# Down-projection products in another order, a buffer of its own for a weight sum, eight raw weight buffers, and gate/up low parts on VectorE instead of by DMA

## The chip, the cores and the metric

The kernel runs on one core of a Trainium2 chip. The metric is the device time of one execution in microseconds, taken as the median of several runs. The engines are TensorE (PE in the profile, its weight loads PEld), VectorE (DVE), ScalarE (ACT), GpSimd (POOL) and SyncE (SP); each runs its own instructions strictly in the order in which they stand in the program.

## The reference

The model is a trunk of two layers over 512 tokens of width 1024. A layer is a half-weighted SwiGLU block (FFN), a token-mixing block, and another FFN. Only the FFN is touched by the change:

```
def swiglu(x, w_gate_up, w_down):
    g, u = jnp.split(x @ w_gate_up, 2, axis=-1)
    return (jax.nn.silu(g) * u) @ w_down

x = x + 0.5 * swiglu(rms_norm(x, ffn1_norm[l]), ...)     # 1024 -> 2 x 2816 -> 1024
x = x + token_mixing(rms_norm(x, mix_norm[l]), ...)
x = x + 0.5 * swiglu(rms_norm(x, ffn2_norm[l]), ...)
```

The work is done to float32 accuracy: a product of two float32 matrices is made of three matmuls in a reduced format, high part by high part, high by low, and low by high.

## The kernel before

**Who orders the instructions.** A scheduler in Python runs when the kernel is built. Every piece of work is a task that yields instructions with a priority and a guessed cost and waits for events; the scheduler simulates the engines and writes each engine's instructions in the order of its simulation. On the chip that order is fixed; semaphores are put in from the tiles that instructions read and write.

**Weights.** `Stream` brings all weights of the FFNs and of the mix stage as units of 128x1024. SyncE loads a unit into one of RAWB raw buffers (`wraw`), and it is cut into a high part `whi` and a low part `wlo`, for which there are CUTB = 3 pairs of buffers. A pair comes free when TensorE has done the product that uses it, a raw buffer when the unit has been cut. For a gate/up or mix unit ScalarE writes the negative of the raw weights, rounded to the reduced format, into `wlo` (L357) and the high part into `whi` (L358), and GpSimd issues a DMA that adds the raw weights to `wlo` (L359). For a unit of the down-projection ScalarE makes the high part (L363) and VectorE subtracts it from the raw weights (L364).

**An FFN.** The 22 chunks of 128 hidden columns are done in three blocks of 8, 8 and 6 (`BLOCKS`). For a chunk, gate and up are 8 x 3 matmuls of 128x512 each into a bank psa (L502 to L504). After a block its part of the down-projection follows: two quads, q0 and q1, each for four of the eight output tiles of x. A quad is a two-by-two block product by the Strassen-Winograd scheme: seven products p0 to p6 instead of eight, each of one weight unit (weights or sums of weights) with one *form* of the hidden pairs. A pair is two chunks; the forms of a pair (`Pair.make`) are cut into high and low parts in the order 0, then 3 and 4, 5 and 6, and last 2 and 1. A product takes, for each of the 4 (in the third block 3) pairs, 6 matmuls of 128x256 (L693, L695, L696). The products accumulate in three banks: z in pst, y in pso, x in pss. Since the sums of the scheme nest, z is used by four products one after the other and is read after each.

**The weight sums.** `sums` and `third` make the combinations of the four weight quarters: a GpSimd DMA adds one quarter to another in a raw buffer (L302, L319), VectorE adds two buffers (L306, L311).

**Reading the accumulators** (`evac` in `down`). ScalarE copies the accumulators of the first three products (L761, L767, L771) and so lets the next product use the bank; VectorE adds the copies to x (L756). The last four are added from PSUM directly (L756 too). After the last block each finished x tile starts the next norm: high part by ScalarE (L555), low part by VectorE (L556), square by ScalarE, sum of squares on GpSimd (L572).

Of the kernel before, what the change touches and what calls it, by code (L numbers as in the profile page):

```python
# [12 lines left out]
F32 = mybir.dt.float32  # L13
# [7 lines left out]
P = 128  # L21
S = 512
# [16 lines left out]
           gc=9288)  # L39
RAWB, CUTB = 6, 3  # L40
NSLOT = 58
# [18 lines left out]
NHU = PLAN.count("s")  # L60
QUADS = [e for e in PLAN if e != "s"]

# [34 lines left out]
class Event:  # L97
    def __init__(self):
        self.done = False
        self.waiting = []  # L100
# [127 lines left out]
class Unit:  # L228


    def __init__(self, w=1024, plain=None):
        self.w, self.plain = w, plain
        self.src, self.ev = Event(), Event()
        self.raw = self.hi = self.lo = None


class Stream:
# [5 lines left out]
    def __init__(self, nc, sch, pool, wall, wq):  # L243
        self.nc, self.s, self.pool, self.wall, self.wq = nc, sch, pool, wall, wq
        self.order, self.avail = [], 0
        self.raw, self.cut = Res(RAWB), Res(CUTB)
        self.units, self.plain, self.quads = [], [], {}
        for e in PLAN:
            if e == "s":
                u = Unit(plain=len(self.plain))  # L250
                self.plain.append(u)
                self.units.append(u)
            else:
                self.quads[e] = [Unit(quad_width(e)) for _ in range(7)]
                self.units += self.quads[e]

    def task(self, gate):
        self.s.spawn(self._cutter(), -1e6)
        n = 0
        for e in PLAN:  # L260
            if e == "s":
# [32 lines left out]
    def _quad(self, e):  # L294
        i, w = QUADS.index(e), quad_width(e)
        u11, us1, us2, u12, us3, us4, u22 = self.quads[e]
        w11, w12, w21, w22 = (self.wq[i, k][:, :w] for k in range(4))
        V, O, s, prio = self.nc.vector, self.nc.gpsimd, self.s, -1e6 + 10 * i

        def sums(t11, t22, t12):  # L300
            yield 1.0
            yield "pool", 0.9, lambda: O.dma_start(t22, w21, accum_op=ALU.add), {}  # L302
            yield 5.0
            s.set(us1.src)
            yield us1.ev
# [3 lines left out]
            yield us2.ev  # L309
            yield u12.ev  # L310
            yield DVE(w, lambda: V.tensor_add(t22, t22, t12), ap=1)  # L311
            s.release(self.raw)
            s.set(us4.src)
            yield us4.ev
            s.release(self.raw)

        def third(t11):
# [3 lines left out]
            s.set(us3.src)  # L321
            yield us3.ev
            s.release(self.raw)

        def last():
            yield u22.ev
# [7 lines left out]
        s.spawn(sums(u11.raw, us1.raw, u12.raw), prio)  # L334
        u22.raw = yield from self._load(w22)
        self._later(u22.src, 2.0)
        s.spawn(last(), prio)

# [8 lines left out]
    def _cut(self, k, u):  # L347
        A, V, O = self.nc.scalar, self.nc.vector, self.nc.gpsimd
        if u.plain == 0:
            for i in range(4):  # L350
# [4 lines left out]
                yield 0.6  # L355
        elif u.plain is not None:
            yield ACT(u.w, lambda: A.mul(u.lo, u.raw, -1.0))  # L357
# [4 lines left out]
        else:  # L362
            yield ACT(u.w, lambda: A.copy(u.hi, u.raw))  # L363
            yield DVE(u.w, lambda: V.tensor_sub(u.lo, u.raw, u.hi.bitcast(F32)), ap=1)  # L364
        if u.plain is not None:
            self.s.release(self.raw)
# [26 lines left out]
def trunk_kernel(ctx: ExitStack, tc: tile.TileContext, wall, wq, x_in, pos_in, cols_in, out):  # L393
# [235 lines left out]
    class Pair:  # L629
# [8 lines left out]
        def make(self, a, b):  # L638
# [14 lines left out]
            for src, i, j in ((t, 3, 4), (u, 5, 6), (b, 2, 1)):  # L653
# [7 lines left out]

    STEPS = ((0, 0, "z", True), (1, 3, "y", True), (2, 5, "z", False), (3, 1, "x", True), (4, 4, "z", False),
             (5, 2, "y", False), (6, 6, "z", False))

    def quad(e, pairs, evac, prio):
# [7 lines left out]
        def product(i):  # L673
            iu, form, z, begin = STEPS[i]
            u, H = units[iu], S // 2
            before = [j for j in range(i) if STEPS[j][2] == z]
            yield u.ev
# [31 lines left out]
    def ffn(name, l, u, xs, nxt):  # L709
# [38 lines left out]
        def down(b, q, was, prio):  # L748
# [9 lines left out]
            def evac(acc, done, seen):  # L758
                q1, q5, uu = G(), G(), G()
                yield done[0]  # L760
                yield ACT(S, lambda: A.copy(q1, acc["z"]))  # L761
                sch.set(seen[0])
                for ev in was:
                    yield ev
                yield add(x11, q1, 0.5)
                yield done[1]
                yield ACT(S, lambda: A.copy(q5, acc["y"]))  # L767
                sch.set(seen[1])
                yield add(x22, q5, -0.5)
                yield done[2]  # L770
                yield ACT(S, lambda: A.copy(uu, acc["z"]))  # L771
                sch.set(seen[2])
                yield add(x12, uu, 0.5)
                yield done[3]
                yield add(x11, acc["x"], 0.5, bump=EVAC)
                sch.release(banks[QBANK["x"]])
                yield done[4]
                yield add(x22, acc["z"], -0.5, bump=EVAC)
                sch.set(seen[4])
                yield done[5]  # L780
                yield add(x12, acc["y"], 0.5, bump=EVAC)
                sch.release(banks[QBANK["y"]])
                last = b == len(BLOCKS) - 1
                for r in range(2):
                    m = 4 * q + r
                    if last:
                        sch.set(new[m][1])
                        nxt.add(m, new[m][0], prio + r)
                yield done[6]
                yield add(x21, acc["z"], -0.5, bump=EVAC)  # L790
                sch.release(banks[QBANK["z"]])
                for r in range(2, 4):
                    m = 4 * q + r
                    if last:
                        sch.set(new[m][1])
                        nxt.add(m, new[m][0], prio + r)

# [44 lines left out]
    def mix(l, u, xs, nxt):  # L842
# [11 lines left out]
        def v_task():  # L854
            kinds = ["a", "a", "t", "o"]
            for k in range(KT - 1):
                yield u.u[k].ev
# [28 lines left out]
            for t in range(NB):  # L886
                p = vp[t]
                p.h = gp.tile([P, 256], F32R, name="vh", tag="vh", bufs=NB)
                p.lo = gp.tile([P, 256], F32R, name="vl", tag="vl", bufs=NB)
                rt = u.tok[:, t:t + 1]  # L890
# [512 lines left out]
```

## Time and the profile before

| | before |
|---|---|
| median of 3 runs | 2984.92 us (2982.92 to 2985.18) |
| profiled execution | 2984.55 us, span 2982.8 us |
| TensorE busy | 2874.0 us, 96% |
| ScalarE busy | 1541.4 us, 52% |
| VectorE busy | 1430.8 us, 48% |
| GpSimd busy | 791.6 us, 27% |
| mean granted TensorE clock | 0.984 of full speed |

The profiled execution is one of many and lies within the spread of the runs. Busy times are sums over the span. A matmul counts as busy until its modelled end, which overlaps the start of the next. The clock is a share of 2.4 GHz; the granted levels are 1.2 and 2.4 GHz.

### The profile page before, as it was taken

The page shows a single profiled execution, that of the slowest core. Times are in us where ns is not written, and L with a number is a line of the kernel's source. Part 1 is how long each engine was busy: PE and PEld are TensorE (multiplying, and loading weights), DVE is VectorE, ACT ScalarE, POOL GpSimd, SP SyncE. Part 2 cuts the span into 40 slices and gives each one's busy share as a digit, 9 for nine tenths or more (in the row PEclk, how much of TensorE's full clock was granted, in tenths as well). Part 3 has the DMA queues.
Part 4 walks back from the last instruction along what each step waited for, and adds up shares of the span by engine and source line. Part 5 has one row for each costly group of instructions (what it writes and reads, how often), then busy time and mean ns, then how long its engine had stood idle before and what let it go on. Part 6 is the DMA issues. An engine that isn't in the chain of part 4 may idle for free.

```text
span 2982.8 us, 36980 instructions
## 1 busy us (share of the span) xinstructions
PE 2874.0 (96%) x14304; PEld 2407.7 (81%) x14304; DVE 1430.8 (48%) x2371; ACT 1541.4 (52%) x2076; POOL 791.6 (27%) x795
## 2 busy tenths in 40 slices
PE   8999989899999999999999999999999999999997
PEld 6888878678888888888878888877788888888886
DVE  5835568954313223535635356599352221235545
ACT  5544457666534455444454444566665334544444
POOL 2111155633222231111220111646242222311111
PEclk9999999899999999999999999998999999999998
DMA  8686677576688888687686865866757888877773
GB/s 218 161 195 167 150 186 162 131 158 155 141 189 189 187 191 186 162 180 171 145 186 167 186 170 136 205 139 141 162 135 163 186 193 184 190 179 171 172 182 84
DMA packets 141233, 503.51 MB, mean 169 GB/s; under 512 B 15681, under 2 KB 16321, under 8 KB 141057
## 3 DMA queue, kind: packets, MB, share of 16 engines
q0 software_dynamic: 65600, 236.75, 43.9%
q1 hardware_dynamic: 74736, 263.23, 28.1%
q8 instruction: 113, 1.85, 0.3%
q10 hardware_dynamic: 720, 1.17, 0.1%
q14 instruction: 64, 0.52, 0.1%
HBM read 285.60 MB, written 2.10 MB: 96 GB/s over the span
## 4 chain that ended last, share of the span: by engine, by line
PE 78%; DVE 11%; issue 6%; DMA 3%; POOL 1%; ACT 1%; SPq 0%; DVEq 0%; POOLq 0%; ACTq 0%
PE psa L504 23%; PE psa L502 22%; PE psa L503 22%; DMA wlo<-wraw 3%; DVE g L949 2%; DVE m L948 2%; PE pst L693 1%; PE pst L696 1%; PE pst L695 1%; DVE g L1034 1%; DVE g L974 1%; DVE wlo L364 1%; DVE g L1014 1%; PE pso L696 1%; DVE wraw L306 1%
## 5 line engine op out<-in xcount | busy, mean ns | idle before, releaser
L502 PE MATMUL psa<-g,whi 128*128 128x512 f32 x3216 | 1283.4, 399 | 37.9 <-DVE xr L969 15.5
L504 PE MATMUL psa<-g,wlo 128*128 128x512 f32 x3216 | 1280.6, 398 | 20.2 <-DMA wlo<-wraw 20.2
L503 PE MATMUL psa<-g,whi 128*128 128x512 f32 x3216 | 1278.7, 398 | 0.3 <-DVE g L556 0.3
L357 ACT ACTIVATE wlo<-wraw 128x1024 fp32r<-128x1024 f32 x407 | 431.4, 1060 | 911.4 <-PE psa L504 860.7
L502 PEld LDWEIGHTS psa<-g,whi 128*128 128x128 f32 x3216 | 611.0, 190 | 185.7 <-DVE xr L969 9.2
L504 PEld LDWEIGHTS psa<-g,wlo 128*128 128x128 f32 x3216 | 610.6, 190 | 171.3 <-DMA wlo<-wraw 26.4
L503 PEld LDWEIGHTS psa<-g,whi 128*128 128x128 f32 x3216 | 610.7, 190 | 140.9 <-DVE g L556 1.3
L359 POOL DMA_DIRECT2D wlo<-wraw x407 | 353.6, 869 | 1319.6 <-ACT wlo L357 1207.7
L358 ACT CAST whi<-wraw 128x1024 fp32r<-128x1024 f32 x407 | 420.8, 1034 | 0.0
L363 ACT CAST whi<-wraw 128x1024 fp32r<-128x1024 f32 (+1 forms) x168 | 159.8, 977 | 228.4 <-PE psa L503 97.1
L693 PE MATMUL pst<-g,whi 128*128 128x256 f32 x704 | 203.7, 289 | 18.9 <-ACT g L761 17.1
L696 PE MATMUL pst<-g,wlo 128*128 128x256 f32 x704 | 200.7, 285 | 5.7 <-DVE wlo L364 5.7
L695 PE MATMUL pst<-g,whi 128*128 128x256 f32 x704 | 200.9, 285 | 0.0
L364 DVE TENSOR_TENSOR wlo<-wraw,whi 128x1024 fp32r<-128x1024 f32 (+1 forms) x168 | 186.1, 1133 | 29.0 <-ACT whi L363 28.9
L733 DVE TENSOR_TENSOR g<-psa,g 128x512 f32<-128x512 f32 x88 | 60.8, 691 | 252.7 <-PE psa L504 252.5
L724 DVE TENSOR_TENSOR g<-psa,g 128x512 f32<-128x512 f32 x88 | 60.8, 691 | 235.7 <-PE psa L504 235.6
L693 PEld LDWEIGHTS pst<-g,whi 128*128 128x128 f32 x704 | 134.9, 192 | 25.0 <-ACT g L761 20.2
L696 PEld LDWEIGHTS pst<-g,wlo 128*128 128x128 f32 x704 | 135.0, 192 | 6.5 <-DVE wlo L364 6.5
L695 PEld LDWEIGHTS pst<-g,whi 128*128 128x128 f32 x704 | 135.2, 192 | 0.6
L656 DVE TENSOR_TENSOR g<-g 128x512 fp32r<-128x512 f32 x132 | 90.8, 688 | 47.5 <-ACT g L655 47.5
L319 POOL DMA_DIRECT2D wraw<-in_wq_dram x24 | 20.8, 867 | 345.0 <-DVE wraw L306 192.2
L696 PE MATMUL pso<-g,wlo 128*128 128x256 f32 x352 | 100.1, 284 | 5.9 <-DVE wlo L364 5.9
(222 smaller groups left out, 3258.8 us busy)
## 6 DMA issues: line engine op xcount, KB each, us to landing
wraw<-in_w_dram SPq DMA_DIRECT2D x407, 512.0 KB, 4.5
wlo<-wraw POOLq DMA_DIRECT2D x407, 512.0 KB, 5.9
wraw<-in_wq_dram SPq DMA_DIRECT2D x64, 512.0 KB, 4.6
wraw<-in_wq_dram POOLq DMA_DIRECT2D x32, 512.0 KB, 7.0
wraw<-in_wq_dram SPq DMA_DIRECT2D x32, 384.0 KB, 3.5
wraw<-in_wq_dram POOLq DMA_DIRECT2D x16, 384.0 KB, 5.7
x<-in_x_dram SPq DMA_DIRECT2D x8, 256.0 KB, 4.7
out_dram<-g ACTq DMA_DIRECT2D x4, 256.0 KB, 2.9
```

Of the source, the lines that this page charges most:

```text
L357: yield ACT(u.w, lambda: A.mul(u.lo, u.raw, -1.0))
L358: yield ACT(u.w, lambda: A.copy(u.hi, u.raw))
L359: yield "pool", 0.9, lambda: O.dma_start(u.lo, u.raw, accum_op=ALU.add), {}
L363: yield ACT(u.w, lambda: A.copy(u.hi, u.raw))
L364: yield DVE(u.w, lambda: V.tensor_sub(u.lo, u.raw, u.hi.bitcast(F32)), ap=1)
L502: T.matmul(ps, wh, xh, start=first, stop=False)
L503: T.matmul(ps, wh, xl, start=False, stop=False)
L504: T.matmul(ps, wl, xh, start=False, stop=last)
L656: yield DVE(S, lambda: V.tensor_sub(lo, src, h.bitcast(F32)))
L693: T.matmul(o, u.hi[:, c], xh, start=begin and k == 0 and m == 0, stop=False, skip_group_check=True)
L695: T.matmul(o, u.hi[:, c], xl, start=False, stop=False, skip_group_check=True)
L696: T.matmul(o, u.lo[:, c], xh, start=False, stop=k == n - 1 and m == 1, skip_group_check=True)
```

## The change

There are four parts. The raw buffers become eight. Plan letters tell mix units ("m", cut as before) from gate/up units ("s"), whose low part VectorE now subtracts (L365 of the kernel after, L364 is ScalarE's copy) with no DMA. The sum of three weight quarters gets a raw buffer of its own, and the units of a quad are cut in another order. The products run in the order of forms 0, 1, 5, 3, 4, 2, 6 on the accumulators z, x, z, y, z, y, z, and no accumulator is copied: VectorE adds each from PSUM in the order of the products (L759 after), and the next product on that bank follows the add. Besides, the parts of V share one slot, and the task that makes V waits for one part of the norm fewer.

```diff
-RAWB, CUTB = 6, 3
+RAWB, CUTB = 8, 3
...
         if _part == "mix":
-            PLAN += ["s"] * 116
+            PLAN += ["m"] * 116
...
-        u11, us1, us2, u12, us3, us4, u22 = self.quads[e]
+        u11, u12, us2, us1, us3, us4, u22 = self.quads[e]
...
-        def sums(t11, t22, t12):
+        def sums(t11, t22, t12, ts):
             yield 1.0
             yield "pool", 0.9, lambda: O.dma_start(t22, w21, accum_op=ALU.add), {}
             yield 5.0
             s.set(us1.src)
-            yield us1.ev
-            yield DVE(w, lambda: V.tensor_add(t22, t22, t11), ap=1)
+            yield DVE(w, lambda: V.tensor_add(ts, t22, t11), ap=1)
             s.set(us2.src)
             s.spawn(third(t11), prio + 1)
+            s.spawn(freed(us1), prio)
             yield us2.ev
+            yield DVE(w, lambda: V.tensor_add(ts, ts, t12), ap=1)
+            s.set(us4.src)
...
-        us1.raw = us2.raw = us4.raw = yield from self._load(w22)
+        us1.raw = yield from self._load(w22)
+        yield self.raw
+        us2.raw = us4.raw = self.pool.tile([P, 1024], F32, name="wraw", tag="wraw", bufs=RAWB)[:, :w]
...
-        elif u.plain is not None:
+        elif u.dma:
             yield ACT(u.w, lambda: A.mul(u.lo, u.raw, -1.0))
             yield ACT(u.w, lambda: A.copy(u.hi, u.raw))
             yield "pool", 0.9, lambda: O.dma_start(u.lo, u.raw, accum_op=ALU.add), {}
...
         else:
             yield ACT(u.w, lambda: A.copy(u.hi, u.raw))
             yield DVE(u.w, lambda: V.tensor_sub(u.lo, u.raw, u.hi.bitcast(F32)), ap=1)
...
-    STEPS = ((0, 0, "z", True), (1, 3, "y", True), (2, 5, "z", False), (3, 1, "x", True), (4, 4, "z", False),
-             (5, 2, "y", False), (6, 6, "z", False))
+    STEPS = ((0, "z", True), (1, "x", True), (5, "z", False), (3, "y", True), (4, "z", False), (2, "y", False),
+             (6, "z", False))
...
-                q1, q5, uu = G(), G(), G()
-                yield done[0]
-                yield ACT(S, lambda: A.copy(q1, acc["z"]))
-                sch.set(seen[0])
...
+                for i, z, outs, final in todo:
+                    yield done[i]
+                    for dst, f in outs:
+                        yield add(dst, acc[z], f, bump=EVAC)
+                    sch.set(seen[i])
+                    if final:
+                        sch.release(banks[QBANK[z]])
...
-            for k in range(KT - 1):
+            for k in range(KT - 2):
                 yield u.u[k].ev
```

The rows below stand in the built programs of the two kernels; numbers behind names tell buffers apart.

The first place is the first quad of the second block (layer 0, first FFN), VectorE before: `g_111` to `g_113` are ScalarE's copies of accumulators, `wlo_2197`, `wlo_2243`, `wlo_2267` and `wlo_2280` are the low parts of the fourth to seventh unit.

```order
L364 TENSOR_TENSOR wlo_2197<-wraw_1956,whi_2196 128x1024
L656 TENSOR_TENSOR g_2214<-g_2175,g_2213 128x512
L311 TENSOR_TENSOR wraw_1922<-wraw_1922,wraw_1956 128x1024
L656 TENSOR_TENSOR g_2239<-g_2132,g_2238 128x512
L364 TENSOR_TENSOR wlo_2243<-wraw_1880,whi_2242 128x1024
L364 TENSOR_TENSOR wlo_2267<-wraw_1922,whi_2266 128x1024
L756 SCALAR_TENSOR_TENSOR x1_95<-g_112,x1_95 128x2x256
L364 TENSOR_TENSOR wlo_2280<-wraw_1994,whi_2279 128x1024
L756 SCALAR_TENSOR_TENSOR x0_94<-g_113,x0_94 128x2x256
L756 SCALAR_TENSOR_TENSOR x0_94<-pss_2231,x0_94 128x2x256
L756 SCALAR_TENSOR_TENSOR x1_95<-pst_2133,x1_95 128x2x256
```

VectorE after, the same quad: `wlo_2159`, `wlo_2163` and `wlo_2176` are the low parts of the fifth to seventh unit, `wraw_1944` is the next quad's sum, and the adds from pss and pst are those of p1 and p2.

```order
L659 TENSOR_TENSOR g_2150<-g_2027,g_2149 128x512
L365 TENSOR_TENSOR wlo_2159<-wraw_1677,whi_2158 128x1024
L306 TENSOR_TENSOR wraw_1944<-wraw_1896,wraw_1866 128x1024
L365 TENSOR_TENSOR wlo_2163<-wraw_1745,whi_2162 128x1024
L365 TENSOR_TENSOR wlo_2176<-wraw_1825,whi_2175 128x1024
L759 SCALAR_TENSOR_TENSOR x0_94<-pss_2055,x0_94 128x2x256
L759 SCALAR_TENSOR_TENSOR x0_94<-pst_2028,x0_94 128x2x256
L759 SCALAR_TENSOR_TENSOR x1_95<-pso_2116,x1_95 128x2x256
```

The adds of copies are gone; the adds of p1 and p2 now stand behind three low parts of later products and the other quad's sum.

TensorE after, in this quad: the end of p1 (pss) and the first matmuls of p4 (pst, with `wlo_2159`).

```order
L696 MATMUL pss_2055<-g_2149,whi_2000 128x256
L698 MATMUL pss_2055<-g_2150,whi_2000 128x256
L699 MATMUL pss_2055<-g_2149,wlo_2001 128x256
L696 MATMUL pst_2028<-g_1574,whi_2158 128x256
L698 MATMUL pst_2028<-g_1575,whi_2158 128x256
L699 MATMUL pst_2028<-g_1574,wlo_2159 128x256
```

Before, p5 on pso stood behind the end of p3 on pss, and p4 behind p5; now p4 on pst follows p1 directly. In the kernel after, p3 and the last pair of p2 end ahead of these rows, in that order: 12 matmuls, six of p2 and six of p1, lie between the end of p3 and p4.

The second place is a stretch of gate/up units early in the first FFN, ScalarE before.

```order
L357 ACTIVATE wlo_571<-wraw_340 128x1024
L358 CAST whi_570<-wraw_340 128x1024
L357 ACTIVATE wlo_613<-wraw_381 128x1024
L358 CAST whi_612<-wraw_381 128x1024
L726 ACTIVATE g_607<-g_607 128x512
```

ScalarE after, at about the same place.

```order
L364 CAST whi_490<-wraw_264 128x1024
L364 CAST whi_534<-wraw_276 128x1024
L729 ACTIVATE g_529<-g_529 128x512
L477 ACTIVATE sq_90<-g_496 128x512
L364 CAST whi_578<-wraw_288 128x1024
```

One of two instructions per unit is gone from ScalarE; its place is taken by one on VectorE (L365), and GpSimd issues no DMA for such a unit. There are 175 of these units.

## Rows read from the trace of the kernel before

**Rows 1.** The page: the span, and busy time of each engine.

```profile
span 2982.8 us, 36980 instructions
...
PE 2874.0 (96%) x14304; PEld 2407.7 (81%) x14304; DVE 1430.8 (48%) x2371; ACT 1541.4 (52%) x2076; POOL 791.6 (27%) x795
```

**Rows 2.** TensorE's waits: releaser, sum in us, times, longest.

```profile
PE psa L504 <- DMA wlo<-wraw: 20.2, 13, 4.8
PE pst L693 <- ACT g L761: 17.1, 8, 4.2
...
PE pso L696 <- DVE wlo L364: 5.9, 8, 0.7
PE pst L696 <- DVE wlo L364: 5.7, 4, 1.4
...
PE pst L693 <- ACT g L771: 1.2, 4, 0.3
```

**Rows 3.** TensorE's waits from 105 to 391 us, the same columns.

```profile
PE psa L504 <- DMA wlo<-wraw: 1.1, 2, 0.7
```

**Rows 4.** Single waits of TensorE in the timeline: start, us, instruction, idle before it.

```profile
17.21 0.50 PE L502 MATMUL psa<-g,whi 128*128 128x512 f32 x1 [2.69 <-ACT g L555]
...
21.82 0.79 PE L504 MATMUL psa<-g,wlo 128*128 128x512 f32 x1 [2.35 <-DMA wlo<-wraw]
...
377.05 0.54 PE L693 MATMUL pst<-g,whi 128*128 128x256 f32 x1 [4.14 <-ACT g L761]
...
384.78 0.39 PE L696 MATMUL pst<-g,wlo 128*128 128x256 f32 x1 [1.42 <-DVE wlo L364]
...
1493.47 0.79 PE L504 MATMUL psa<-g,wlo 128*128 128x512 f32 x1 [2.43 <-DMA wlo<-wraw]
...
2949.62 0.39 PE L693 MATMUL pst<-g,whi 128*128 128x256 f32 x1 [1.87 <-ACT g L761]
```

**Rows 5.** Timeline of TensorE at 259 us, block 1, first quad.

```profile
259.27 0.28 PE L693 MATMUL pst<-g,whi 128*128 128x256 f32 x1
...
259.87 0.28 PE L696 MATMUL pst<-g,wlo 128*128 128x256 f32 x1
259.99 0.28 PE L693 MATMUL pso<-g,whi 128*128 128x256 f32 x1
```

**Rows 6.** Timeline of VectorE, the same place.

```profile
255.55 1.22 DVE L364 TENSOR_TENSOR wlo<-wraw,whi 128x1024 fp32r<-128x1024 f32 x1
256.69 0.68 DVE L756 SCALAR_TENSOR_TENSOR x<-g,x 128x512 f32<-128x512 f32 x1
257.29 0.68 DVE L756 SCALAR_TENSOR_TENSOR x<-pss,x 128x512 f32<-128x512 f32 x1
260.19 0.69 DVE L756 SCALAR_TENSOR_TENSOR x<-pst,x 128x512 f32<-128x512 f32 x1 [2.22 <-PE pst L696]
```

**Rows 7.** Timeline of ScalarE, the same place.

```profile
260.07 1.05 ACT L363 CAST whi<-wraw 128x1024 fp32r<-128x1024 f32 x1 [4.46 <-PE pst L695]
```

**Rows 8.** Groups of VectorE by line and shape, 105 to 391 us.

```profile
L364 DVE TENSOR_TENSOR wlo<-wraw,whi 128x768 fp32r<-128x768 f32 x14 | 12.9, 951 | 0.0
```

**Rows 9.** Stretches: length, busy us of PE, PEld, DVE, ACT, POOL; clock; DMA share; GB/s.

```profile
373.50:377.10 3.60, 0.05 (x1) 0.05 (x1) 3.60 (x5) 2.67 (x5) 1.30 (x3) 1.00 0.26 20
377.10:380.50 3.40, 3.40 (x16) 3.40 (x17) 3.40 (x4) 0.38 (x1) 1.41 (x1) 0.50 0.51 94
384.70:388.10 3.40, 3.32 (x28) 3.32 (x29) 2.46 (x4) 1.12 (x2) 0.00 (x0) 1.00 0.69 214
2950.80:2954.20 3.40, 3.40 (x18) 3.40 (x17) 2.12 (x4) 1.24 (x2) 0.00 (x0) 0.50 0.55 97
18.70:25.50 6.80, 4.45 (x12) 2.97 (x11) 3.71 (x3) 4.62 (x8) 5.02 (x4) 0.50 1.05 215
```

**Rows 10.** VectorE at 372 us, last block, second quad.

```profile
372.30 2.02 DVE L306 TENSOR_TENSOR wraw<-wraw 128x768 f32<-128x768 f32 x1
```

**Rows 11.** GpSimd at the same time.

```profile
370.25 3.25 POOL L572 TENSOR_TENSOR g<-g 128x512 f32<-128x512 f32 x2 [18.99 <-ACT g L563]
```

More of the change, by code (lines that the diff above doesn't have):

```diff
@@ L59 @@
                 PLAN += ["s"] * (2 * (_c1 - _c0)) + [(_part, _l, _b, _q) for _q in range(2)]
-NHU = PLAN.count("s")
-QUADS = [e for e in PLAN if e != "s"]
+NHU = sum(isinstance(e, str) for e in PLAN)
+QUADS = [e for e in PLAN if not isinstance(e, str)]
 def quad_width(e):
@@ L228, with __init__ @@
 class Unit:
-    def __init__(self, w=1024, plain=None):
-        self.w, self.plain = w, plain
+    def __init__(self, w=1024, plain=None, dma=False):
+        self.w, self.plain, self.dma = w, plain, dma
         self.src, self.ev = Event(), Event()
@@ L248, in __init__ @@
         for e in PLAN:
-            if e == "s":
-                u = Unit(plain=len(self.plain))
+            if isinstance(e, str):
+                u = Unit(plain=len(self.plain), dma=e == "m")
                 self.plain.append(u)
@@ L260, in task @@
         for e in PLAN:
-            if e == "s":
+            if isinstance(e, str):
                 if n == 1:
@@ L304, in sums @@
             s.set(us1.src)
-            yield us1.ev
-            yield DVE(w, lambda: V.tensor_add(t22, t22, t11), ap=1)
+            yield DVE(w, lambda: V.tensor_add(ts, t22, t11), ap=1)
             s.set(us2.src)
             s.spawn(third(t11), prio + 1)
+            s.spawn(freed(us1), prio)
             yield us2.ev
+            yield DVE(w, lambda: V.tensor_add(ts, ts, t12), ap=1)
+            s.set(us4.src)
+            s.spawn(freed(us4), prio)
             yield u12.ev
[L311 to L314, printed above, removed]
             s.release(self.raw)
@@ L321, in third, with freed @@
             s.set(us3.src)
[L322 to L326, printed above, removed]
+            yield from freed(us3)
+        def freed(u):
+            yield u.ev
             s.release(self.raw)
@@ L330, in _quad @@
         self._later(u11.src, 2.0)
-        us1.raw = us2.raw = us4.raw = yield from self._load(w22)
+        us1.raw = yield from self._load(w22)
+        yield self.raw
+        us2.raw = us4.raw = self.pool.tile([P, 1024], F32, name="wraw", tag="wraw", bufs=RAWB)[:, :w]
         u12.raw = yield from self._load(w12)
         self._later(u12.src, 2.0)
-        s.spawn(sums(u11.raw, us1.raw, u12.raw), prio)
+        s.spawn(sums(u11.raw, us1.raw, u12.raw, us2.raw), prio)
         u22.raw = yield from self._load(w22)
         self._later(u22.src, 2.0)
-        s.spawn(last(), prio)
+        s.spawn(freed(u22), prio)
     def _cutter(self):
@@ L364, in _cut @@
             yield DVE(u.w, lambda: V.tensor_sub(u.lo, u.raw, u.hi.bitcast(F32)), ap=1)
+            if u.plain is not None:
+                self.avail += 8
         if u.plain is not None:
@@ L673, in product @@
         def product(i):
-            iu, form, z, begin = STEPS[i]
-            u, H = units[iu], S // 2
-            before = [j for j in range(i) if STEPS[j][2] == z]
+            form, z, begin = STEPS[i]
+            u, H = units[i], S // 2
+            before = [j for j in range(i) if STEPS[j][1] == z]
             yield u.ev
@@ L763, in evac @@
                 for ev in was:
                     yield ev
[L765 to L796, printed above, removed]
+                for i, z, outs, final in todo:
[5 more added lines that the diff above has]
+                        sch.release(banks[QBANK[z]])
+                    if i >= 5 and b == len(BLOCKS) - 1:
+                        for r in range(2 * (i - 5), 2 * (i - 4)):
+                            m = 4 * q + r
+                            sch.set(new[m][1])
+                            nxt.add(m, new[m][0], prio + r)
@@ L887, in v_task @@
                 p = vp[t]
-                p.h = gp.tile([P, 256], F32R, name="vh", tag="vh", bufs=NB)
-                p.lo = gp.tile([P, 256], F32R, name="vl", tag="vl", bufs=NB)
+                v = G(F32R)
+                p.h, p.lo = v[:, :256], v[:, 256:]
                 rt = u.tok[:, t:t + 1]
```

3 lines of the change are left out of this document (added).

## The prediction

> **What bounds the kernel now.** I read the page first: TensorE is busy 2874.0 of 2982.8 us, VectorE under half [rows 1]. So every gain or loss is a change in TensorE's idle time or in its clock. The list of its waits comes next: from it the reader is to take that the waits this change touches are many and short [rows 2]. The list for one FFN alone separates them from those of the mix stage, which the change leaves nearly as it is [rows 3]. Then single waits in the timeline [rows 4], the pace of the engines in the first quad of a block [rows 5 to 7], and the windows behind long waits, for the clock [rows 9].
>
> Three readings are used throughout. Six 128x256 matmuls start 0.72 us apart (259.27 to 259.99), so one takes 0.12 [rows 5]. The last one's record ends at 259.87 + 0.28 = 260.15, 0.16 after the next has started; an idle time of the profile is counted from such an end, so each wait costs 0.16 more than its number. VectorE's instructions also overlap a little: a low part takes 1.22 but the next starts 1.14 later, and an add starts 0.60 before its successor [rows 6]. The engines take over from TensorE's last matmul quickly: with the following one at 259.99, ScalarE's copy began at 260.07 and VectorE's add at 260.19, 0.08 and 0.20 later [rows 5 to 7].
>
> The clock: the 3.4 us after the idle 4.14 us at 377.05 were run at 0.50 of full speed (the 1.2 GHz level), as were 3.4 us after the 1.87 us at 2949.62; after 1.42 us idle at 384.78 it stayed at 1.00 [rows 4, 9]. A stretch of 3.4 us at half speed does 1.7 us of work, so it costs 1.7.
>
> **What the change removes.** (1) ScalarE's three copies of accumulators and the waits on them, and the old product order in which weights came late: all the waits of the down-projections, on L761 17.1, on L771 1.2, on L364 5.9 and 5.7, are 29.9 us in 24 waits [rows 2], with 24 x 0.16 = 33.7. I take all of it: what replaces these waits is priced below. (2) The DMA that makes a gate/up low part. TensorE waits for it twice per FFN, 1.1 us [rows 3], so 4.4 in four, at the start of a layer's first FFN 2.35 and 2.43 [rows 4]; 9.2 in ten waits, with 0.16 each 10.8. In its place stands one VectorE instruction of 1.14 behind one ScalarE copy of 1.05, 2.3 us for a unit of 24 matmuls that TensorE needs over 5 us for. VectorE takes 175 of them, some 200 us more on 1430.8 of 2982.8, so it does not become the bound. The rest of the 20.2 us, lies in the mix stage, whose units stay with the DMA; I count nothing. (3) Half of ScalarE's work for a gate/up unit. Once that shows: at 17.21 TensorE waits 2.69 for the cut of the norm, and one instruction of about 1.0 before it goes; I take 1.0. (4) The clock that those waits cost. Each FFN's last block has one long wait on L761 (4.14 in the first, 1.87 in the last [rows 4]; 17.1 for all eight leaves room for two more like the first), and the 2.43 at 1493.47 is another: 5 x 1.7 = 8.5. Of the 6.8 us at half speed after 18.7 [rows 9] I take half as gone, 1.7. Together: 33.7 + 10.8 + 1.0 + 10.2 = 55.7 us. The bounds: nothing at the start (-2.7), all of its slow stretch (+1.7).
>
> Eight raw buffers and the sum's own buffer cost and bring nothing by themselves: no load is among the waits in rows 2. A buffer more is held per quad, two more exist. If a load did come late, a quad's first sum would, and the wait is then one more of the kind below.
>
> **What it adds.** Now the accumulator z is used by p0, p2, p4, p6, and each of these must wait until VectorE has added the one before from PSUM. Before, ScalarE's copy released it. In the first quad of a block the adds stand in product order, that of p1 ahead of that of p2, while TensorE ends p2 before p1, since p1's last pair needs the form made last. The order of VectorE shows what is queued between: the low part of the fifth unit, the next quad's first sum, the low parts of the sixth and seventh unit, the add of p1, the add of p2. The low parts want cut buffers that p3, p2 and p1 free by ending. TensorE has nothing but p4 next, which waits for that last add.
>
> For seven of the eight first quads of four pairs, from the end of p3: copy begins 0.08, takes 1.05, hand-over 0.03 (estimate, from the 0.08), four VectorE instructions of 1.14 = 4.56, add 0.60, add 0.69, hand-over 0.06 (same estimate): 7.07. TensorE still has 12 matmuls of p2 and p1, 1.43. It stands 5.64 us. For the four first quads of three pairs the instructions are narrower (0.951 busy, so 0.87 start to start, and 0.85 for the copy by the same ratio [rows 8]); the add of p1 comes after the first low part: 0.08 + 0.85 + 0.03 + 4 x 0.87 + 0.60 + 0.69 + 0.06 = 5.79, less 1.43 is 4.36. In the kernel's very first quad both adds stand ahead: p4 waits 0.20 + 0.60 + 0.69 + 0.06 = 1.55, then for its low part, which ends 0.20 + 1.20 + 1.14 + 1.22 + 0.06 = 3.82 after p1, so 3.6 in all. Sum 7 x 5.64 + 4 x 4.36 + 3.6 = 60.5.
>
> p2 has the same wait on p0's add, 0.20 + 0.69 + 0.06 = 0.95; in the seven quads six matmuls of another product (0.72) cover it: 7 x 0.23 + 5 x 0.95 = 6.4. In the second quads adds and low parts alternate on VectorE, all forms are there, and six or more matmuls of 18 or 24 lie between two products on z: nothing. Without that cover each would cost 0.95, 11.4 in twelve.
>
> The clock falls after each of the twelve waits, if 3.6 to 5.6 us idle do what 1.87 and 4.14 did: 12 x 1.7 = 20.4. Added: 60.5 + 6.4 + 20.4 = 87.3. What the stall itself delays, the low parts of the sixth and seventh unit, is done before p4 ends; nothing further is late.
>
> Does the subtraction run at 1.14 everywhere? At 372.30 the sum L306 over two SBUF inputs took 2.02 instead of about 0.95 while GpSimd added squares [rows 8, 10, 11]. The Trainium skill says so ("SBUF — State Buffer", section "SBUF: two separate sides"): a VectorE instruction with two SBUF inputs and a GpSimd instruction that reads SBUF exclude each other for their whole length. By it the sum would lose in the last blocks alone, where GpSimd adds squares in the second quad; 1.07 us for one instruction in each of four is 4.3, and I leave it out, since before has such pairs at the same place; it counts in the range.
>
> **Sum.** 87.3 - 55.7 = +31.6. The profiled execution took 2984.55 (its span 2982.8), the median of the runs is 2984.92; so 2984.55 + 31.6 = 3016 us, about 1.1% more. What a measurement of this kernel can tell from no change is 0.2%, 6 us.
>
> **Rivals.** *A: the adds are not late and only the gains remain.* The point that decides is the twelve waits of p4: the change is even when they, their clock and p2's waits come to 55.7, 4.6 us a quad against my 7.3. It needs p1 to end well before p2's add is due, or VectorE to reach the add before the three low parts. For it: VectorE is busy 48% of the span [rows 1]. Against: an engine runs its row of instructions in order, and three of those ahead of the add wait for TensorE's own products. Time: 2984.55 - 55.7 + 6.4 = 2935 us. The Trainium skill speaks for this outcome ("Perfetto Trace Analysis", section "Matmuls"): matmul groups that rotate through PSUM banks let the evacuation of one overlap the next. No row here shows four products that do so on one accumulator. Chance 0.10.
>
> *B: the waits come but the clock holds.* It stayed up over 1.42 us, and two rows of falls are few. Then 87.3 - 20.4 - 55.7 = +11.2: 2996 us. Against: all my waits of p4 are longer than the 1.87 us that brought a fall [rows 4, 9]; in the very first quad the 3.6 is split, though. Chance 0.10, half of it within 0.2% if some 5 us more are lost from my sum.
>
> *C: the slow stretch is longer.* At 18.7 it lasted 6.8 us [rows 9]; with that, 12 x 1.7 more and 4.3 for GpSimd's exclusion: +56.3, 3041 us. Chance 0.13.
>
> **How the numbers follow.** My own case, 0.67, has the waits as worked out and one slow stretch each; its terms move by some 10 us to either side (a tenth on 60.5, the bounds of the start, 4.3 of exclusion, 11.4 if the second quads wait too): 3006 to 3030. The range takes in nearly all of B and most of what lies between my case and C: 2992 to 3037. Faster by over 0.2%: A, 0.10. Within: half of B and a little of what lies between A and B, 0.06. Slower: 0.84.
>
> **What would show it.** Right: in the first quad of each block one TensorE wait of 5.6 us (3.6 in the first, 4.4 in the third blocks) on an accumulator's add, half clock behind it, and a VectorE row without idle time before that add; no wait of gate/up on a DMA; none of the down-projection on ScalarE; no 4 us wait in the second quad of the last block. Wrong: if VectorE stands idle in that chain, or TensorE waits there under 2 us. I would be wrong too if the new subtractions of gate/up delay the adds that free TensorE's banks for gate/up.

## The result, and the profile after

The changed kernel took 3033.65 us (median of four runs, 3031.31 to 3036.49), the kernel before 2983.99 beside it: a ratio of 1.0167 with an interval of 1.0149 to 1.0184. That is 50 us more, where 31.6 were forecast; the time lies in the range, near its upper end. The profiled execution of the changed kernel took 3036.49 us, with a span of 3034.6.

The page of the kernel after, span and busy times, to be read against [rows 1]:

```profile
span 3034.6 us, 36600 instructions
...
PE 2897.2 (95%) x14304; PEld 2432.5 (80%) x14304; DVE 1629.6 (54%) x2546; ACT 1344.5 (44%) x1829; POOL 638.6 (21%) x620
```

TensorE has the same 14304 matmuls. VectorE is busy 199 us more and ScalarE 197 us less, close to the 200 us that the forecast took for the 175 low parts, and no engine but TensorE is near the span. The list of TensorE's waits (releaser, sum in us, times, longest) answers to [rows 2]:

```profile
PE pst L696 <- DVE x L759: 64.0, 20, 5.6
...
PE psa L507 <- DMA wlo<-wraw: 9.3, 5, 3.1
...
PE pss L595 <- POOL g L575: 5.7, 3, 3.4
...
PE pso L699 <- DVE wlo L365: 2.0, 4, 0.6
...
PE pst L699 <- DVE wlo L365: 1.7, 1, 1.7
```

None of the old waits of the down-projections is left: no ScalarE copy releases TensorE there. One new line has taken their place, the add of an accumulator (L759), 64.0 us. The five waits on the DMA, 9.3 us, all lie in the mix stages. The same waits singly, in the timeline of TensorE: p2 behind p0's add at 112.85 and p4's low part at 123.17 in the very first quad, and p4 behind p2's add at 260.86 in block 1, the place that the forecast worked out; the last row is spoken of with the experiments.

```profile
112.85 0.38 PE L696 MATMUL pst<-g,whi 128*128 128x256 f32 x1 [0.78 <-DVE x L759]
...
123.17 0.58 PE L699 MATMUL pst<-g,wlo 128*128 128x256 f32 x1 [1.70 <-DVE wlo L365]
...
260.86 0.55 PE L696 MATMUL pst<-g,whi 128*128 128x256 f32 x1 [5.61 <-DVE x L759]
...
1520.65 0.37 PE L595 MATMUL pss<-ones,g 128*128 128x1 f32 x1 [1.87 <-POOL g L575]
```

What VectorE and ScalarE did in those 5.61 us, in their timelines (start, duration, instruction; `x2` and `x3` are runs of the same one):

```profile
254.88 1.23 DVE L365 TENSOR_TENSOR wlo<-wraw,whi 128x1024 fp32r<-128x1024 f32 x1 [1.90 <-ACT whi L364]
256.02 1.22 DVE L306 TENSOR_TENSOR wraw<-wraw 128x1024 f32<-128x1024 f32 x1
257.16 2.35 DVE L365 TENSOR_TENSOR wlo<-wraw,whi 128x1024 fp32r<-128x1024 f32 x2
259.43 0.69 DVE L759 SCALAR_TENSOR_TENSOR x<-pss,x 128x512 f32<-128x512 f32 x1
260.03 0.68 DVE L759 SCALAR_TENSOR_TENSOR x<-pst,x 128x512 f32<-128x512 f32 x1
```

```profile
253.79 1.05 ACT L364 CAST whi<-wraw 128x1024 fp32r<-128x1024 f32 x1 [1.62 <-issue]
```

The reader is to see a row without a gap: low part of the fifth unit, the other quad's sum, two low parts, the add of p1, the add of p2. It starts when p3's end has freed a pair of cut buffers and ends 0.15 before TensorE's p4. The next matmul behind p3 started at 253.67; forecast was p4 at 253.67 + 7.07 = 260.74, measured 260.86.

The clock, in windows of the kernel after (length, busy us of PE, PEld, DVE, ACT, POOL, then the granted clock, DMA share, GB/s), beside [rows 9]:

```profile
255.30:258.70 3.40, 0.00 (x0) 0.00 (x0) 3.40 (x4) 1.44 (x2) 0.00 (x0) 1.00 0.47 112
258.70:265.50 6.80, 4.64 (x22) 4.67 (x23) 2.61 (x4) 0.00 (x0) 0.00 (x0) 0.50 0.55 178
371.40:378.20 6.80, 5.46 (x25) 5.49 (x26) 3.03 (x5) 0.83 (x1) 0.00 (x0) 0.50 0.44 154
1628.00:1630.90 2.90, 2.90 (x14) 2.90 (x14) 0.44 (x1) 0.00 (x0) 0.00 (x0) 0.50 0.65 256
23.20:30.00 6.80, 6.80 (x24) 5.93 (x25) 2.06 (x6) 2.53 (x3) 0.00 (x0) 0.50 0.41 117
1518.20:1528.40 10.20, 8.33 (x28) 6.88 (x27) 3.42 (x8) 2.53 (x3) 2.32 (x2) 0.50 0.13 37
```

The first window is the wait itself, with TensorE idle and the clock still at 1.00. The clock fell at 258.7, 2.2 us before the wait ended, and stayed at 0.50 (1.2 GHz) for 6.8 us, not 3.4; at 371.4 likewise. Only what TensorE worked in such a stretch counts: half of 4.64 and of 5.46, 2.3 and 2.7 us. Eleven of the twelve first quads have a stretch of 6.8 us and one (the fourth row shows it from the moment work began) of 3.4.

### The profile page after: what moved, and what is told of

It is laid out like the page before. It is cut to its first block, busy times and chain, and to the rows that moved or that the text cites. A ratio compares the mean times of both kernels' runs of the same rounds, so it can differ in the third digit from the quotient of the medians.

```text
span 3034.6 us, 36600 instructions
## 1 busy us (share of the span) xinstructions
PE 2897.2 (95%) x14304; PEld 2432.5 (80%) x14304; DVE 1629.6 (54%) x2546; ACT 1344.5 (44%) x1829; POOL 638.6 (21%) x620
## 3 DMA queue, kind: packets, MB, share of 16 engines
q1 hardware_dynamic: 74736, 263.23, 27.5%
## 4 chain that ended last, share of the span: by engine, by line
PE 82%; DVE 11%; issue 3%; DMA 1%; ACT 1%; POOL 1%; SPq 0%; DVEq 0%; POOLq 0%; ACTq 0%
PE psa L507 22%; PE psa L505 22%; PE psa L506 22%; PE pst L696 3%; PE pst L699 3%; PE pst L698 3%; DVE g L932 2%; DVE m L931 1%; DVE wlo L365 1%; DMA wlo<-wraw 1%; PE pso L696 1%; PE pso L698 1%; PE pso L699 1%; DVE g L1017 1%; DVE x L759 1%
## 5 line engine op out<-in xcount | busy, mean ns | idle before, releaser
L364 ACT CAST whi<-wraw 128x1024 fp32r<-128x1024 f32 (+1 forms) x343 | 345.8, 1015 | 898.5 <-PE psa L506 440.0
L507 PEld LDWEIGHTS psa<-g,wlo 128*128 128x128 f32 x3216 | 610.6, 190 | 158.0 <-DMA wlo<-wraw 12.6
L358 ACT ACTIVATE wlo<-wraw 128x1024 fp32r<-128x1024 f32 x232 | 245.7, 1059 | 475.7 <-PE psa L507 462.1
L365 DVE TENSOR_TENSOR wlo<-wraw,whi 128x1024 fp32r<-128x1024 f32 (+1 forms) x343 | 410.4, 1200 | 44.8 <-ACT whi L364 44.0
L360 POOL DMA_DIRECT2D wlo<-wraw x232 | 201.8, 870 | 500.1 <-ACT wlo L358 486.5
L696 PE MATMUL pst<-g,whi 128*128 128x256 f32 x704 | 212.3, 302 | 64.5 <-DVE x L759 64.0
L359 ACT CAST whi<-wraw 128x1024 fp32r<-128x1024 f32 x232 | 240.1, 1035 | 0.0
L698 PE MATMUL pst<-g,whi 128*128 128x256 f32 x704 | 209.1, 297 | 0.0
L696 PEld LDWEIGHTS pst<-g,whi 128*128 128x128 f32 x704 | 143.5, 204 | 71.2 <-issue 59.1
L319 POOL DMA_DIRECT2D wraw<-in_wq_dram x24 | 20.6, 859 | 748.6 <-DVE wlo L365 748.6
L303 POOL DMA_DIRECT2D wraw<-in_wq_dram x24 | 24.6, 1025 | 653.5 <-DMA wraw<-in_wq_dram 326.2
L699 PEld LDWEIGHTS pst<-g,wlo 128*128 128x128 f32 x704 | 143.7, 204 | 1.9 <-DVE wlo L365 1.9
L698 PEld LDWEIGHTS pst<-g,whi 128*128 128x128 f32 x704 | 143.9, 204 | 1.0
L658 ACT CAST g<-g 128x512 fp32r<-128x512 f32 x132 | 77.5, 615 | 87.0 <-DVE g L653 74.7
```

What stands on the lines that cost most here:

```text
L360: yield "pool", 0.9, lambda: O.dma_start(u.lo, u.raw, accum_op=ALU.add), {}
L507: T.matmul(ps, wl, xh, start=False, stop=last)
L658: yield ACT(S, lambda: A.copy(h, src))
L696: T.matmul(o, u.hi[:, c], xh, start=begin and k == 0 and m == 0, stop=False, skip_group_check=True)
L698: T.matmul(o, u.hi[:, c], xl, start=False, stop=False, skip_group_check=True)
L699: T.matmul(o, u.lo[:, c], xh, start=False, stop=k == n - 1 and m == 1, skip_group_check=True)
```

## The experiments

All are written from the kernel after, but for one from the kernel before. Each was timed beside the kernel before on the same chip, whose median there was 2984.63 to 2985.68 us. In the lists of waits z is pst, y is pso and x is pss.

**The add of p2 ahead of the add of p1.** One pair is exchanged in the list that orders the adds.

```diff
-        todo = ((0, "z", ...), (1, "x", ...), (2, "z", ...), (3, "y", ...), ...
+        todo = ((0, "z", ...), (2, "z", ...), (1, "x", ...), (3, "y", ...), ...
```

> The kernel after, with one line changed: the add of p2 stands ahead of that of p1 on VectorE. If the place of that add in VectorE's row makes the loss (my theory), the add comes out ahead of the three low parts: p4 then waits about 0.2 us for the add and 0.9 us for its own low part in each first quad instead of 5.6 or 4.3, no clock falls there, and the time drops by some 60 to 75 us to about 2965 us. If VectorE as a whole is too loaded by the gate/up low parts, or the weights come late, the waits only change their name and the time stays within 10 us of 3034.

Measured: 2990.57 us, 1.0014 of before (1.0004 to 1.0023); 43 us of the 50 are gone, fewer than the 60 to 75 expected.

```profile
PE pso L696 <- DVE x L759: 19.7, 11, 1.8
...
PE pst L699 <- DVE wlo L365: 8.3, 12, 3.2
...
PE pst L696 <- DVE x L759: 7.2, 15, 0.9
```

The waits of z on adds fall from 64.0 to 7.2 us. So the place of one add in VectorE's row made the long stalls, with the same load on VectorE and the same weights. Two shorter waits show in their stead, which the stall had covered: p5's on the add of p3, still behind the low parts (19.7), and p4's on its own low part (8.3).

**ScalarE's copies for z after p0 and p2.**

```diff
+                    if i in (0, 2):
+                        src = G()
+                        yield ACT(S, lambda: A.copy(src, acc[z]))
+                        sch.set(seen[i])
```

> The kernel after, but ScalarE copies z after p0 and p2 as before, and the next product waits for the copy instead of the add. By my theory the waits of p4 and p2 on adds vanish; about 0.8 us for the low part of p4's own unit stays in each first quad, and the time is about 2955 us. By the rival that the new order of products itself (which unit is cut when) makes the loss, the time stays above 3010.

Measured: 3001.00 us, 1.0053 (1.0036 to 1.0070), between the two expectations. The waits, and ScalarE in block 1:

```profile
PE pst L696 <- ACT g L773: 25.8, 17, 2.5
...
PE pso L699 <- DVE wlo L365: 13.8, 4, 4.1
PE pso L696 <- DVE x L759: 9.7, 10, 1.1
```

```profile
250.25 2.94 ACT L364 CAST whi<-wraw 128x1024 fp32r<-128x1024 f32 x3 [1.55 <-issue]
```

The stall of 5.6 us goes, so the order of products as such does not make it; but 2955 was too low. z now waits 25.8 us for ScalarE: the copy of p2's accumulator stands behind three instructions that make high parts (the row above), and p4 waits 2.01 us for it there. It is the same mechanism in another engine's row. Products on y wait 23.5 us for low parts and adds.

**Gate/up low parts by the DMA again.**

```diff
-                u = Unit(plain=len(self.plain), dma=e == "m")
+                u = Unit(plain=len(self.plain), dma=len(self.plain) > 0)
```

> The kernel after, but the low parts of gate/up units are made by GpSimd's DMA as before, so that VectorE has 175 instructions fewer. By my theory the waits of p4 stay at 5.6 and 4.4 us, since the row ahead of the add is the same, and the waits on that DMA come back, about 11 us: some 3045 us. By the rival that VectorE is too loaded the waits of p4 shrink by half or more and the time falls under 3015.

Measured: 3041.36 us, 1.0185 (1.0170 to 1.0200).

```profile
PE pst L696 <- DVE x L759: 67.3, 19, 5.6
PE psa L507 <- DMA wlo<-wraw: 16.9, 10, 3.7
...
PE pss L595 <- POOL g L575: 3.4, 1, 3.4
```

With 175 instructions fewer on VectorE the waits for the add are as long as before the edit. VectorE's load is not the cause. The low parts on VectorE are worth 3041.36 - 3033.65 = 7.7 us, though the two intervals overlap.

The waits of p4 are no shorter than in the kernel after, but only seven of the twelve stretches at half clock last 6.8 us here; five last 3.4. One of the five, behind a wait of 5.60 us that ends at 1383.03, and the stretch after it, with the clock at 1.00 again:

```profile
1382.70:1386.00 3.30, 2.97 (x14) 3.00 (x15) 0.78 (x2) 0.00 (x0) 0.00 (x0) 0.50 0.71 284
1386.10:1389.40 3.30, 3.30 (x30) 3.30 (x29) 1.63 (x2) 1.05 (x1) 0.00 (x0) 1.00 0.02 5
```

**The old products and the old reading, the rest of the change kept.** The order of units and of products and the function that reads the accumulators are those of before.

```diff
-        u11, u12, us2, us1, us3, us4, u22 = self.quads[e]
+        u11, us1, us2, u12, us3, us4, u22 = self.quads[e]
...
-    STEPS = ((0, "z", True), (1, "x", True), (5, "z", False), (3, "y", True), ...
+    STEPS = ((0, "z", True), (3, "y", True), (5, "z", False), (1, "x", True), ...
```

> The kernel after, but with the order of products, of the units in a quad, and the reading of accumulators of before (ScalarE's copies); eight raw buffers, the sum's own buffer and the low parts on VectorE stay. By my theory this keeps most of the gains and loses nothing: 2930 to 2950 us, faster than before by 35 to 55. By the rival that the gains are not there (the waits on the DMA and on ScalarE's copies only move), it lies within 10 us of 2984.

Measured: 2979.10 us, 0.9981 (0.9972 to 0.9990). Faster than before, so the loss lies in what was undone; but by 6 us, not by 35 to 55. A new wait has taken up most of the gain:

```profile
PE pss L699 <- DVE wlo L365: 24.4, 16, 4.1
```

The place in block 1, VectorE and then TensorE:

```profile
244.48 1.22 DVE L306 TENSOR_TENSOR wraw<-wraw 128x1024 f32<-128x1024 f32 x1
245.61 1.22 DVE L365 TENSOR_TENSOR wlo<-wraw,whi 128x1024 fp32r<-128x1024 f32 x1
```

```profile
246.89 0.39 PE L699 MATMUL pss<-g,wlo 128*128 128x256 f32 x1 [0.94 <-DVE wlo L365]
```

With a buffer of its own and eight raw buffers the next quad's first sum (L306) is ready early, and the scheduler puts it ahead of the low part for p3, for which TensorE then stands. In the kernel after the same instruction lies inside the long chain. The sum ahead of that low part goes with half of the new wait, 11.9 us in twelve first quads. The other 12.6 us are four waits in the second quads of the third blocks. The longest of them, a low part of VectorE ahead of it, and GpSimd at that time:

```profile
374.07 0.58 PE L699 MATMUL pss<-g,wlo 128*128 128x256 f32 x1 [4.06 <-DVE wlo L365]
```

```profile
367.47 2.05 DVE L365 TENSOR_TENSOR wlo<-wraw,whi 128x768 fp32r<-128x768 f32 x1
```

```profile
367.33 1.38 POOL L575 TENSOR_TENSOR g<-g 128x512 f32<-128x512 f32 x1 [2.76 <-ACT g L566]
```

The low part took 2.05 us instead of 0.95 while GpSimd added squares, the lengthening that the forecast saw at 372.30 [rows 8, 10, 11]. Later instructions in that row grew likewise.

**Matmuls that only fill the wait.** Ahead of p4 in each first quad TensorE gets 36 matmuls (24 with three pairs) into a spare bank that nobody reads; n is the number of pairs.

```diff
+            if i == 4 and e[3] == 0:
+                for j in (1, 2, 3):
+                    yield done[j]
+                yield banks["s"]
...
+                yield PE((12 * n - 12) * 262, fill)
```

> The kernel after, with idle matmuls put into TensorE's row behind p1 and ahead of p4 in every first quad: 36 of 128x256 (24 in the third blocks), about 4.3 and 2.9 us of work into a bank that nobody reads, so that they lie inside the wait for the add. If the clock's fall is a cost of its own (my account gives the twelve falls 28 us of the 50), the falls in the first quads go, the add comes no later, and the time drops by some 20 to 28 us to about 3008 us. If the clock costs little and the wait itself is all, the time stays at 3034 within 5.

Measured: 3008.01 us, 1.0076 (1.0061 to 1.0091), 25.6 us less than the kernel after, though TensorE does more work. Windows at the first quads of blocks 1 and 2, and the wait of p4:

```profile
255.00:262.00 7.00, 5.73 (x49) 5.56 (x48) 4.34 (x6) 0.78 (x1) 0.00 (x0) 1.00 0.63 212
366.00:380.00 14.00, 12.07 (x101) 11.72 (x99) 11.07 (x14) 8.35 (x13) 3.64 (x3) 1.00 0.40 104
```

```profile
PE pst L708 <- DVE x L771: 20.7, 19, 1.4
```

The clock holds 1.00 through both quads, and no first quad of this run has a fall; the wait that is left is what the filling leaves over. p4 starts as late as in the kernel after: in both traces 7.2 us after the matmul that follows p3, with three pairs 5.9. So about half of the loss was the clock: 25.6 us of it is bought back without moving an add in VectorE's row. The size is good to a few us, since falls outside the first quads differ between the two traces too, by 5.7 us of lost work.

**Forms 2 and 1 made early.**

```diff
-            for src, i, j in ((t, 3, 4), (u, 5, 6), (b, 2, 1)):
+            for src, i, j in ((b, 2, 1), (u, 5, 6), (t, 3, 4)):
```

> The kernel after, with the forms of a pair made in the order 0, then 2 and 1, 5 and 6, 3 and 4, so that p1 ends first and p3 last of the three. VectorE's row then has the adds of p1 and p2 ahead of the low parts by themselves. By my theory the waits of p4 shrink to about 1 us and the time to that of the swapped adds, about 2990 us; a part of the wait moves to p5, which wants the add of p3, queued behind the low parts. By the rival that the swap helped only because p1's bank was freed later, the time stays near 3034.

Measured: 2983.52 us, 0.9995 (0.9985 to 1.0004): the same as before.

```profile
PE pso L696 <- DVE x L759: 14.0, 12, 1.2
...
PE pst L696 <- DVE x L759: 6.1, 8, 1.0
```

p1 now ends before p2, both adds stand ahead of the low parts without a change to their order, and the wait of z on adds is 6.1 us; p5 waits 14.0 us for the add of p3. Two edits of different places that both bring the add forward remove the stall; the rival that p1's bank mattered has nothing left, since p1's bank is freed later in the one and earlier in the other.

**The low parts alone, on the kernel before.** Gate/up units take the branch that quads have; nothing else changes.

```diff
-        elif u.plain is not None:
+        elif u.dma:
...
             yield DVE(u.w, lambda: V.tensor_sub(u.lo, u.raw, u.hi.bitcast(F32)), ap=1)
+            if u.plain is not None:
+                self.avail += 8
```

> The kernel before with one part of the change alone: the low parts of gate/up units on VectorE (six raw buffers, old products, old reading of accumulators). By the terms of my sum for this part (10.8 for the waits on the DMA, 1.0 at the start, 1.7 to 3.4 of clock) 2969 to 2973 us. The kernel with old products but eight buffers and the sum's own buffer measured 2979; if those two cost something by moving the next quad's first sum ahead of the first quad's low parts, this one is faster than that; if they are free, it lies at 2979 too.

Measured: 2977.33 us, 0.9973 (0.9964 to 0.9983): 7.3 us, less than the 12 to 16 of my sum, and 1.8 us from the kernel with the old products, which cannot be told apart from it. Eight raw buffers and the sum's own buffer together thus bring or cost nothing that shows in the time.

```profile
PE psa L506 <- DMA wlo<-wraw: 9.4, 2, 4.7
...
PE pss L594 <- POOL g L574: 5.9, 3, 3.4
```

The waits on the DMA in the FFNs are gone (the two left are of the mix stage), but a wait on GpSimd's squares has grown from one to three times, as in the kernel after. There its longest new member is the row of 1520.65 above, 1.87 us, inside a stretch at half clock of 10.2 us (the window from 1518.2). With the DMA's low parts that line of waits is one again, 3.4 us.

**Four pairs of cut buffers, six raw buffers.**

```diff
-RAWB, CUTB = 8, 3
+RAWB, CUTB = 6, 4
```

> The kernel after, with four pairs of cut buffers and six raw buffers, which take the same space. The low part of p4 is then made ahead of time, and the one that stands ahead of the add wants no buffer of p2 any more; the scheduler also puts 18 matmuls of the next quad's p0 between p1 and p4. If the buffers that p3, p2 and p1 free are what holds VectorE's row (my theory), the wait of p4 falls from 5.6 to some 1 to 3 us, mostly filled, and the time lies near 2990 us. If the number of low parts in the row alone sets it, the wait for the add stays over 4 us and the time over 3015.

Measured: 2995.20 us, 1.0037 (1.0023 to 1.0052).

```profile
PE pst L696 <- ACT whi L364: 16.1, 13, 1.5
PE pst L699 <- DVE wlo L365: 15.6, 12, 2.2
...
PE pst L696 <- DVE x L759: 4.2, 10, 2.0
```

ScalarE and VectorE in block 1:

```profile
254.60 1.05 ACT L364 CAST whi<-wraw 128x1024 fp32r<-128x1024 f32 x1 [3.16 <-PE pso L698]
```

```profile
255.69 3.50 DVE L365 TENSOR_TENSOR wlo<-wraw,whi 128x1024 fp32r<-128x1024 f32 x3 [2.73 <-ACT whi L364]
```

The waits of z on adds are 4.2 us in all, but this does not tell the buffers from the number of low parts. Three low parts still stand ahead of the two adds in block 1, and they still begin when the end of p3 lets ScalarE make a high part (254.60). The 18 matmuls of the next quad cover the wait, and TensorE stands for weights instead: 31.7 us in the first two lines. What the run shows is that VectorE's row hangs on a buffer that p3 frees, and that the kernel with other work in between is 38 us faster than the kernel after.

**Three mixtures.** Early forms with ScalarE's copies of p0, p2 and p3; the same with four pairs and six raw buffers; early forms and four pairs without copies. The edits are those above, but for one more copy:

```diff
-                    if i in (0, 2):
+                    if i in (0, 2, 3):
```

> The kernel after with forms 2 and 1 made early (as in the run of that order alone) and ScalarE's copies of the accumulators of p0, p2 and p3. No product then waits for an add in the first quads; about 0.7 us for the low part of p4 is left in each. The run with the forms alone measured 2984; without its 20 us of waits on adds I expect 2965 us, a few less if the copies make no wait of their own, and 2984 if they do.

> The same with four pairs of cut buffers and six raw buffers: the low part of p4 is made early too. By my theory nothing of the first quads' chain is left, and the time is 2950 to 2960 us, the fastest of all; if six raw buffers with the sum's own among them make weights late, TensorE waits for low parts or loads at the second quads and it is no better than 2975.

> The kernel after with forms 2 and 1 made early and four pairs of cut buffers, six raw ones, and no copy: adds from PSUM alone. If a copy is worth only what the low parts ahead of an add cost, this is as fast as the one with copies, 2955 to 2965 us; if an add by itself costs about 0.95 us at each of p2, p4 and p5, some 15 us slower than that.

Measured: 2966.33 us (0.9939, 0.9925 to 0.9954), 2955.03 us (0.9899, 0.9885 to 0.9914), and 2964.25 us (0.9932, 0.9915 to 0.9948), all within what was expected, the third at the upper end. The second is the fastest, 31 us below the kernel before and 79 below the kernel after. Its waits on z, and under them those of the third:

```profile
PE pst L696 <- ACT g L773: 8.1, 12, 0.7
...
PE pst L699 <- DVE wlo L365: 3.4, 3, 1.1
```

```profile
PE pst L696 <- DVE x L759: 14.4, 15, 4.2
```

Without copies the waits of z on adds are 14.4 us, against 8.1 for copies, and the kernel is 9 us slower. Of the 14.4 us 10.2 are three waits in the second quads of third blocks, where low parts stand ahead of the add again; the first of them, TensorE and then VectorE:

```profile
375.57 0.55 PE L696 MATMUL pst<-g,whi 128*128 128x256 f32 x1 [3.02 <-DVE x L759]
```

```profile
372.14 2.69 DVE L365 TENSOR_TENSOR wlo<-wraw,whi 128x768 fp32r<-128x768 f32 x3
```

Everywhere else the adds cost 4.2 us, less than the copies: an add from PSUM is not dearer than a copy where no low part stands ahead of it.

## Why the prediction was right, and where it was off

The direction and the mechanism hold. The size is off, and its fit is in part luck: the 3033.65 us lie outside the 3006 to 3030 of the forecast's own case. They are 18 us from its 3016 and 7 from rival C's 3041, which had a chance of 0.13; the range holds them because it was drawn most of the way to C.

**The stall of p4** was worked out as 5.64 us in seven quads and 4.36 in four. The trace shows 5.59 to 5.61 and 4.31 to 4.32, with the 0.16 that the forecast adds 5.77 and 4.48. The exchanged pair and the early forms each remove it. With 0.16 added for each of 20 waits the line of 64.0 us is 67.2, against 66.9 in the sum (60.5 and 6.4), of which about 2 was for p4's low part in the very first quad, measured as 1.70. **Rival A** (adds not late) did not occur: VectorE's row in block 1 had no gap ahead of the add, and the wait was there in all twelve first quads. The rule of the Trainium skill named there ("Perfetto Trace Analysis", section "Matmuls") speaks of groups that rotate through PSUM banks; z's four products share one bank, so no run here tests it.

**The clock was the term that was mis-sized.** The step "The clock falls after each of the twelve waits ... 12 x 1.7 = 20.4" took one stretch of 3.4 us each, and 10.2 was given back for old falls. Half of what TensorE worked in all stretches at half clock is 36.0 us in the trace of before and 63.5 in that of after: 27.5 more, where 20.4 - 10.2 = 10.2 was forecast. The twelve falls make 29.7 instead of 20.4. Of the 10.2, the four falls behind the old waits on L761 are gone, 6.5 us. But at the start a fall of 6.8 us is still there (TensorE busy through all of it, 3.4 us lost, against 2.2 at 18.7 before [rows 9]), and between the second and third FFN a fall of 10.2 us (8.33 busy, 4.2 lost) stands where one of 3.4 was. A longer stretch is rival C's mechanism; its price of 56.3 was too high, since a part of the longer stretch lies in the wait. The run with filled waits shows the clock's share: 25.6 us.

**TensorE's idle time** grew by 28.5 us (time between two starts beyond that at full clock, where the second had to wait), against 66.9 - 45.5 = 21.4 forecast. Three things in the lists make up much of the 7.1 us. The add waits are a little longer than worked out. The second quads of the third blocks, priced at nothing, have three waits of 0.5 us on adds and three of 0.6 on low parts; there a low part took 2.06 us at 383.78 while GpSimd added squares, the lengthening that the forecast left to its range. And the matmuls with ones now wait three times for GpSimd's squares. This wait was in the change's order and I did not price it: at the kernel's start these matmuls stand behind 45 chunk matmuls of the FFN instead of 60, and between the second and third FFN behind 21 instead of 24. It comes with the low parts on VectorE, since the run that puts the DMA back loses it. Counted by starts the time lost at half clock is 24.7 us more, as a busy time takes in the overlap with the next start; with the 28.5 that is 53.2, against 51.8 us in the two spans.

**The gains were right for this kernel and wrong as gains.** The step "I take all of it" for the 33.7 us of the down-projections holds in the kernel after, where none of these waits is left. It does not hold without the stall: the kernel with the old products had 24.4 us of new waits on low parts, and the one with early forms 14.0 for p5. That the stall covered these is the likely reading; no run shows it for each. The low parts' own 12 to 16 us measured 7.3 on the kernel before and 7.7 on the kernel after. In the trace on the kernel before the idle time fell by 10.9 us, about as summed, but the time lost at half clock rose by 3.1, where 1.7 to 3.4 were to come back.

**Eight raw buffers** were priced at nothing, and the time agrees within 2 us, though they and the sum's own buffer let a sum slip ahead of a low part.

What stays open is what sets the length of a fall. The length of the wait does not: p4's waits of 5.6 us brought stretches of 6.8 and of 3.4 us within one trace, that of the DMA's low parts, and in the same trace a wait of 2.93 us at 544.0 brought none, where 1.87 us had brought one in the kernel before [rows 4, 9]. So eleven long falls of twelve are a property of this trace that the forecast could not have read from its rows. The two changes to V were not run alone.

## What to carry to other kernels

When an accumulator is released by an instruction on an engine with a fixed row, look at what stands ahead of that instruction and what those wait for: here three low parts and a weight sum, the first of which wanted a buffer freed by TensorE's own product, turned a 0.95 us wait for an add into one of 5.6 us, and moving one line undid it. Count the clock with a stall: about half of this loss was work at 1.2 GHz afterwards, and filling the wait with idle matmuls bought it back. A wait that goes can uncover one that it hid, so a gain read from a list of waits is an upper bound until the next one in the chain is priced.

## What the runs showed of the hardware that was not expected

The granted clock fell 2.2 us before the end of a 5.6 us wait, and stayed at half for 6.8 us, of which 4.6 were worked; after the 4.14 us wait of the kernel before it was 3.4 us, from the moment when work began again [rows 4, 9]. Of the twelve waits of p4 eleven brought such a long stretch in the kernel after, seven in the kernel with the DMA's low parts, where the waits are no shorter. Matmuls whose result nobody reads kept the clock at 1.00 through all twelve first quads, with waits of at most 1.4 us left.
